# State contributions of the first token half, formed under the second half's convolution units

## The chip, the core and the metric

The kernel runs on one core of one Trainium2 chip. The core has TensorE for matrix products, VectorE, ScalarE and GpSimd for work on tiles, SyncE for issuing transfers, and sixteen DMA engines. Each engine takes the instructions of its own queue in order; semaphores tie the queues together. The metric is the device time of one execution in microseconds (us).

## The reference

One transformer block: a projection of the normalised tokens, then a pooling mixer beside a bidirectional mLSTM with a short convolution on its queries and keys, then an output projection and a gated feed-forward part. The part that matters here is the recurrent state of the mLSTM and how it is used:

```
px, qx, kx, vx, ox, gx = project(hx, w_in[l], conv_qk[l], gate_bias[l])
pc, qc, kc, vc, oc, gc = project(hc, w_in[l], conv_qk[l], gate_bias[l])
hc_m, st_f, st_b = mlstm_bidir(qc, kc, vc, gc, zero_state(bsz), zero_state(bsz))
hx_m, _, _ = mlstm_bidir(qx, kx, vx, gx, st_f, st_b)
mix_x = jnp.concatenate([pool_x, mlstm_output(hx_m, ox, head_norm[l])], axis=-1) @ w_out[l]
x = x + g1 * mix_x
...
  # per chunk, in mlstm_chunk_scan
  c_new = decay[..., None, None] * c0 + jnp.einsum('bhs,bhsv,bhsd->bhvd', wk, vc, kc)
  n_new = decay[..., None] * n0 + jnp.einsum('bhs,bhsd->bhd', wk, kc)
```

There are 2048 tokens, 256 context tokens, width 1024, 4 heads with keys of 64 and values of 128. All is float32.

## The kernel before, in words

The tokens are worked in chunks of 128: 16 token chunks (0 to 15) and 2 context chunks. What a chunk adds to the states, its *contribution*, does not depend on the states themselves: the values times the weighted keys, one product per head for both directions at once. The states are then linked by a scan over the chunks, once forward and once backward.

The input projection runs in two token halves of 1024 tokens. A *unit* is one 256-column block of the projection for one half, computed by the seven products of a Strassen scheme instead of eight (`unit`, line 648; `product`, line 637: 12 matmuls each, as every operand is split in a high and a low part; the loop order of the products is 0, 1, 4, 3, 5, 2, 6, called A0, A1, A4 and so on below). In the second half four of the seven weight operands are not formed anew: they were kept in DRAM in the first half (`s_w`) and are loaded (line 597). These loads are issued only after the last load of raw weights (`issue_after(raw_last)`, line 596).

The second half runs in this order: pool units; two conv units (keys, then queries; their outputs go to DRAM as `s_k`, `s_q`, line 754); then two *o-units* (output gates), interleaved product by product. For the second o-unit the raw weights go into a tile `rawx` of its own (line 691, 1024 columns).

During the o-units a hook after every product (`chunk_step`) works the state contributions of all 18 chunks, two context chunks first, then token chunks in the order 0, 15, 1, 14, ... For each: a load of keys and values one step ahead (lines 897 and 899), two transposes of the keys on TensorE (line 945), a weighting on VectorE (line 948), four matmuls into PSUM (line 958), four copies of [64, 258] on ScalarE into the state tiles (line 963), and, once a chunk of the upper half is reached, a step of the scan on VectorE (line 968). There are 14 hooks; what is left of the 18 chunks follows behind the units. Then the output weights w_out are loaded, scaled and split for the later projection (lines 978 to 994), partly while the mLSTM loop begins.

The mLSTM loop goes chunk by chunk: keys times queries (line 1090), exponentials of the decay matrix (1097), product with them (1099), outputs `po` from values (1114) and from states (1120), normalisation (1132), loads of pool outputs `pmx` (1146) and output gates `so` (1143), and the projection (1171 to 1173).

The program lines give the logical order; a scheduler then lays each engine's queue out in a fixed order, so that work of several stages is mixed in a queue. A wait at the head of a queue holds up all that stands behind it.

Of the kernel before, what the change touches and what calls it, by code (L numbers as in the profile page):

```python
# [8 lines left out]
F32 = mybir.dt.float32  # L9
# [3 lines left out]
ALU = mybir.AluOpType  # L13
# [8 lines left out]
def tile_hybrid_block(ctx: ExitStack, tc: tile.TileContext, x, c, cx, c_ctx, w_ada, b_ada, norm1, w_in, conv_qk,  # L22
                      gate_bias, pool_w, pool_scale, head_norm, w_out, norm2, w_up, w_down, norm_f, out):
    nc = tc.nc
    P = 128
# [100 lines left out]
    s_g = dram.tile([4, D], F32, name="s_g")  # L126
    s_w = dram.tile([6, 4, 2, P, 512], F32, name="s_w")
    s_e = dram.tile([NCH // 2, P, 512], F32, name="s_e")

# [563 lines left out]
    def run_units(units, psp, wp, tmp, fetch, bg=None):  # L695


        for n, (srcs, sink, after, w, half) in enumerate(units):
            if half:
                make = operands(load_raws(srcs, kept=True), [wp], kept=s_w[w])  # L700
            else:
                make = operands(load_raws(srcs), [wp], keep_=s_w[w])
            A = {}
            for j, i in enumerate(ORDER):
                A[i] = make(i)
                if n == 0 and Btile[j] is None:
                    fetch(j)
            for j, _ in enumerate(unit(A, psp, tmp, sink)):
                if bg and (n, j) in bg:
                    bg.pop((n, j))()  # L710
            after()
# [15 lines left out]
    def conv_unit(bp, half, i0):  # L727
        pre = [bp.tile([P, TH + 3], F32, name=f"pre{r}") for r in range(2)]
        for r in range(2):
            if half == 0:  # L730
                nc.gpsimd.memset(pre[r][:, 1:2], 0.0)
            else:
                nc.gpsimd.tensor_copy(pre[r][:, 0:2], edge[:, i0 + r])
                nc.gpsimd.memset(pre[r][:, TH + 2:TH + 3], 0.0)

        def sink(r, n, ps, sb):
            o = pre[r][:, 2 + n * 512:2 + (n + 1) * 512]
            if sb is None:
                nc.scalar.copy(o, ps)
            else:  # L740
                nc.vector.tensor_tensor(o, ps, sb, op=ALU.add)

        def after():
            for r in (0, 1):
                i = i0 + r
                rows = (s_q, s_k)[i // 2][i % 2 * P:(i % 2 + 1) * P]
                y = bp.tile([P, TH + 1], F32, name="y", bufs=2)
                if half == 0:
                    nc.gpsimd.tensor_copy(edge[:, i], pre[r][:, TH:TH + 2])
                    n, o, t0 = TH - 1, 1, 0  # L750
                else:
                    n, o, t0 = TH + 1, 0, TH - 1
                conv_silu(y[:, :n], pre[r][:, o:], n, conv_w(i), y[:, :n])
                nc.sync.dma_start(rows[:, t0:t0 + n], y[:, :n])
        return in_cols(O_Q + i0 * P), sink, after, i0 // 2, half
# [70 lines left out]
    def o_unit(tmp, half, i0):  # L826
# [8 lines left out]
            nc.scalar.dma_start(s_so[i * P:(i + 1) * P, b * 512:(b + 1) * 512], so)  # L835
        return in_cols(O_O + i0 * P), sink, lambda: None, 4 + i0 // 2, half

    for half in range(2):
        if half:
            Btile = [None] * 7  # L840

        def fetch(j):
            if ORDER[j] < 3:
                load_B(s_hc, j, None, None)
            else:
                load_B(s_ha[half], j, wp, "hst")
        if half == 0:
            padr = ExitStack()
            adr = padr.enter_context(pool("adr2", 1))
            fins = []  # L850

            def acc(seg, n):
                return lambda: fins.append(ada_acc(seg, n, adr, 5))

            def fin():
                fins.pop()(tp, "tp")
            with pool("cvp", 1) as bp:
                run_units([conv_unit(bp, half, i0) for i0 in (2, 0)], pu_, wp, tmp, fetch, {(1, 0): acc(3, 0)})
            with pool("gp", 1) as gp:
                GI = gp.tile([P, P], F32, name="GI")  # L860
                GF = gp.tile([P, P], F32, name="GF")
                gates_to(gat, GI, GF, NCH, 64)


                mask = gat.rearrange("p c g -> p (c g)").rearrange("p (d j) -> p d j", d=2)
                nc.gpsimd.memset(mask, 0.0)
                nc.gpsimd.affine_select(out=mask[:, 0], in_=mask[:, 0], pattern=[[1, P]], compare_op=ALU.is_ge, fill=-BIG, base=0,
                                        channel_multiplier=-1)
                nc.gpsimd.affine_select(out=mask[:, 1], in_=mask[:, 1], pattern=[[-1, P]], compare_op=ALU.is_ge, fill=-BIG, base=0,
                                        channel_multiplier=1)  # L870

                gates = gate_chain(gp, gps, GI, GF, P, NCH, False)
                step = lambda: next(gates, None)
                run_units([o_unit(tmp, half, i0) for i0 in (0, 2)], pu_, wp, tmp, fetch,
                          {(0, 0): step, (0, 2): fin, (0, 3): acc(3, 1), (0, 4): step, (1, 0): step, (1, 2): fin,
                           (1, 3): acc(4, 0), (1, 4): step})
            plp = ExitStack()
            plu = pool_units(plp.enter_context(pool("plp", 1)))
            run_units(plu(0), pu_, wp, tmp, fetch, {(0, 3): fin, (0, 4): acc(4, 1), (1, 5): fin})
        else:  # L880
            run_units(plu(1), pu_, wp, tmp, fetch, {(0, 3): acc(2, 0), (1, 3): fin, (1, 4): acc(2, 1)})
            plp.close()
            rxp = pf.enter_context(pool("rx", 1, "right"))
            with pool("cvp", 1) as bp:
                run_units([conv_unit(bp, half, i0) for i0 in (2, 0)], pu_, wp, tmp, fetch, {(0, 3): fin})
            padr.close()
    tpp.close()

# [6 lines left out]
    def dma_kv(kp, sk, sv, cc, bufs, vp=None):  # L895
        kT = kp.tile([P, 2, P], F32, name="kT", bufs=bufs)
        nc.sync.dma_start(kT, sk[:, cc * P:(cc + 1) * P].rearrange("(t p) c -> p t c", p=P))
        vt = vp.tile([P, 4, 129], F32, name="vta", bufs=2) if vp else vtp.tile([P, 4, 129], F32, name="vt")
        nc.sync.dma_start(vt.rearrange("p h v -> p (h v)"), sv[cc * P:(cc + 1) * P, :])
        return kT, vt  # L900
# [5 lines left out]
    bp = pj.enter_context(pool("pja", 1))  # L906
    tmps = (tmp, bp)

    seq = [(True, cc) for cc in range(NCC)] + [(False, cc) for i in range(NCH // 2) for cc in (i, NCH - 1 - i)]
    todo_kv, loaded = list(seq), []  # L910

    def load_ahead():
        if todo_kv:
            is_ctx, cc = todo_kv.pop(0)
            src = (s_kc, s_vc) if is_ctx else (s_k, s_v)
            kp = bp if not is_ctx and len(todo_kv) < 12 and len(todo_kv) % 4 < 2 else kvp
            loaded.append(dma_kv(kp, *src, cc, 2, kvp if is_ctx or cc in (0, NCH - 1) else None))

    for _ in range(2):
        load_ahead()  # L920
# [15 lines left out]
    def ST(k):  # L936
        return sta[:, TA.index(k)] if k in TA else stb[:, TB.index(k)] if k in TB else stc[:, k - 7]
# [628 lines left out]
```

## Time and profile before

| what | value |
|---|---|
| median of 3 runs | 2119.07 us (2118.11 to 2120.87) |
| profiled execution, its own time | 2117.76 us |
| its span in the profile | 2115.9 us |
| mean granted TensorE clock | 0.982 of full speed |
| busy: TensorE, VectorE, ScalarE, GpSimd | 95%, 65%, 42%, 11% |
| chain that ended last: TensorE, DMA, VectorE, ScalarE | 74%, 11%, 5%, 4% |

The span runs from the first to the last recorded instruction; the execution's own time is 1.9 us more. TensorE is busy for nearly the whole span, so the places where it is not busy are what a change in order can win or lose. The page's slices show the granted clock in tenths; where TensorE is idle for long the clock falls, and it is shown for each stage below.

### The profile page before, as it was taken

How to read it: one execution, taken by the hardware profiler on the slowest of the kernel's cores; microseconds unless marked ns; L12 is line 12 of the kernel's file. 1: busy time of each engine (PE TensorE's matmuls, PEld its weight loads, DVE VectorE, ACT ScalarE, POOL GpSimd, SP SyncE). 2: the span in 40 equal slices, each digit the busy share in tenths (PEclk: the TensorE clock that was granted, in tenths of full speed). 3: DMA queues.
4: the chain of work that ended last, by engine and by line, in shares of the span. 5: the costliest groups of instructions: out<-in, count | busy, mean ns of one | idle time of the engine just before them, and what ended most of it. 6: DMA issues, size and time to landing. Idle time of an engine off the chain costs nothing.

```text
span 2115.9 us, 27589 instructions
## 1 busy us (share of the span) xinstructions
PE 2015.6 (95%) x9482; PEld 1637.0 (77%) x9482; DVE 1365.8 (65%) x2333; ACT 899.1 (42%) x1787; POOL 227.0 (11%) x222
## 2 busy tenths in 40 slices
PE   7999989996999998999999999999999999999998
PEld 3997757775777776788888877888888788888887
DVE  6866868757455566666675588677677554447664
ACT  6643644456444444433333354333333343433442
POOL 1000013211333320000000000000000002004121
PEclk9999999997999999999999999999999999999999
DMA  8598989689586756433342367555565584644642
GB/s 281 169 297 270 301 269 329 219 262 254 138 253 209 241 184 183 140 124 125 100 159 85 100 217 256 189 194 189 174 199 192 190 309 149 226 139 168 226 158 100
DMA packets 365812, 421.42 MB, mean 199 GB/s; under 512 B 23924, under 2 KB 241624, under 8 KB 364904
## 3 DMA queue, kind: packets, MB, share of 16 engines
q1 hardware_dynamic: 319728, 348.22, 50.9%
q10 hardware_dynamic: 45944, 71.43, 10.5%
q8 instruction: 75, 1.23, 0.2%
q14 instruction: 65, 0.53, 0.1%
HBM read 280.45 MB, written 139.12 MB: 198 GB/s over the span
## 4 chain that ended last, share of the span: by engine, by line
PE 74%; DMA 11%; DVE 5%; ACT 4%; issue 3%; SPq 1%; POOL 1%; ACTq 0%; DVEq 0%; POOLq 0%
PE pa L642 8%; PE pa L644 8%; PE pa L643 8%; PE pdn L1392 7%; PE pdn L1393 7%; PE pdn L1394 7%; PE pg L642 4%; PE pg L643 4%; PE pg L644 4%; PE pb L642 2%; PE pb L644 2%; PE pb L643 2%; PE pm L1171 2%; PE pm L1173 2%; PE pm L1172 2%
## 5 line engine op out<-in xcount | busy, mean ns | idle before, releaser
L642 PE MATMUL pa<-h,wh 128*128 128x512 f32 x680 | 271.0, 400 | 7.6 <-ACT p L656 4.7
L644 PE MATMUL pa<-h,wl 128*128 128x512 f32 x680 | 269.8, 397 | 0.3 <-DMA wl<-s_w 0.3
L643 PE MATMUL pa<-h,wh 128*128 128x512 f32 x680 | 269.5, 397 | 0.0
L148 ACT CAST wh<-ws 128x512 fp32r<-128x512 f32 x200 | 123.5, 619 | 281.3 <-PE pg L643 154.2
L1392 PE MATMUL pdn<-ow,op 128*128 128x512 f32 x616 | 236.8, 389 | 1.0 <-ACT op L148 1.0
L1393 PE MATMUL pdn<-ow,op 128*128 128x512 f32 x616 | 237.5, 389 | 0.0
L1394 PE MATMUL pdn<-ow,op 128*128 128x512 f32 x616 | 237.5, 389 | 0.0
L151 DVE TENSOR_TENSOR op<-ra,op 128x512 fp32r<-128x512 f32 x154 | 121.6, 796 | 159.4 <-ACT op L148 159.3
L148 ACT CAST op<-ra 128x512 fp32r<-128x512 f32 x154 | 95.2, 621 | 225.9 <-PE pdn L1394 223.9
L642 PE MATMUL pg<-h,wh 128*128 128x512 f32 x448 | 177.8, 397 | 2.9 <-ACT h L148 1.7
L643 PE MATMUL pg<-h,wh 128*128 128x512 f32 x448 | 178.6, 399 | 0.9 <-DVE h L151 0.8
L644 PE MATMUL pg<-h,wl 128*128 128x512 f32 x448 | 177.5, 396 | 0.0
L151 DVE TENSOR_TENSOR wl<-ws,wh 128x512 fp32r<-128x512 f32 x200 | 136.4, 685 | 55.4 <-ACT wh L148 55.2
L642 PEld LDWEIGHTS pa<-h,wh 128*128 128x128 f32 x680 | 129.0, 190 | 43.2 <-ACT p L656 6.0
L644 PEld LDWEIGHTS pa<-h,wl 128*128 128x128 f32 x680 | 128.5, 189 | 31.1 <-issue 0.5
L643 PEld LDWEIGHTS pa<-h,wh 128*128 128x128 f32 x680 | 128.8, 189 | 30.2 <-issue 1.0
L1424 POOL TENSOR_TENSOR hr<-hr,o 128x1024 f32<-128x1024 f32 x8 | 21.7, 2734 | 1096.7 <-ACT o L1437 927.0
L1392 PEld LDWEIGHTS pdn<-ow,op 128*128 128x128 f32 x616 | 115.6, 188 | 25.5 <-ACT op L148 1.4
L1393 PEld LDWEIGHTS pdn<-ow,op 128*128 128x128 f32 x616 | 115.7, 188 | 23.9
L1394 PEld LDWEIGHTS pdn<-ow,op 128*128 128x128 f32 x616 | 115.7, 188 | 23.9
L613 DVE TENSOR_TENSOR ws<-raw 128x512 f32<-128x512 f32 x100 | 69.0, 690 | 96.3 <-DMA raw<-in_w_up_dram 92.0
L148 ACT CAST vt<-raw 128x512 fp32r<-128x512 f32 x112 | 69.2, 619 | 96.0 <-PE pb L643 41.2
(357 smaller groups left out, 4330.5 us busy)
## 6 DMA issues: line engine op xcount, KB each, us to landing
raw<-in_w_up_dram SPq DMA_DIRECT2D x88, 512.0 KB
ra<-s_act SPq DMA_DIRECT2D x66, 512.0 KB
s_act<-adaw SPq DMA_DIRECT2D x84, 256.0 KB
rwt<-s_t SPq DMA_DIRECT2D x77, 256.0 KB
adaw<-in_w_ada_dram SPq DMA_DIRECT2D x64, 256.0 KB
s_act<-g SPq DMA_DIRECT2D x63, 256.0 KB
s_hb<-hb SPq DMA_DIRECT2D x7, 1792.0 KB
hst<-s_hb ACTq DMA_DIRECT2D x48, 256.0 KB
```

The lines of the kernel that those rows point to most:

```text
L148: nc.scalar.copy(hi, src)
L151: eng_lo.tensor_tensor(lo, src, r32(hi), op=ALU.subtract)
L613: nc.vector.tensor_tensor(t, a, b, op=op)
L642: nc.tensor.matmul(ps, lhsT=ah[:, k], rhs=B[:, 0, k], start=st, stop=False, **kw)
L643: nc.tensor.matmul(ps, lhsT=ah[:, k], rhs=B[:, 1, k], start=False, stop=False, **kw)
L644: mm_last[0] = nc.tensor.matmul(ps, lhsT=al[:, k], rhs=B[:, 0, k], start=False, stop=(k == 3), **kw)
L1171: nc.tensor.matmul(pt, lhsT=mh[:, k], rhs=w[:, 0, k % 4], start=(k == 0), stop=False)
L1172: nc.tensor.matmul(pt, lhsT=mh[:, k], rhs=w[:, 1, k % 4], start=False, stop=False)
L1173: nc.tensor.matmul(pt, lhsT=mlo[:, k], rhs=w[:, 0, k % 4], start=False, stop=(k == 7))
L1392: nc.tensor.matmul(ps, lhsT=A[:, 0, ts_], rhs=W[:, 0], start=start, stop=False)
L1393: nc.tensor.matmul(ps, lhsT=A[:, 0, ts_], rhs=W[:, 1], start=False, stop=False)
L1394: nc.tensor.matmul(ps, lhsT=A[:, 1, ts_], rhs=W[:, 0], start=False, stop=stop)
```

## The change

For the chunks 0 to 6 the contribution is formed earlier, by hooks in the two conv units of the second half, and stored in a DRAM tensor `s_d`. When the later chunk step reaches the mirrored upper chunk, the two halves of the stored contribution are loaded straight into the state tiles. The step list shrinks from 18 to 11: two context chunks, 15 to 9, 7 and 8.

```
+    NE = NCH // 2 - 1
+    s_d = dram.tile([NE, P, 516], F32, name="s_d")
...
+    def early_states(room):
...
+        def load():
+            if todo_e:
+                cc = todo_e.pop(0)
+                kT = room[:, cc % 2 * 256:cc % 2 * 256 + 256].rearrange("p (t c) -> p t c", t=2)
+                nc.sync.dma_start(kT, s_k[:, cc * P:(cc + 1) * P].rearrange("(t p) c -> p t c", p=P))
+                vt = wp.tile([P, 4, 129], F32, name="hst", bufs=3)
+                nc.sync.dma_start(vt.rearrange("p h v -> p (h v)"), s_v[cc * P:(cc + 1) * P, :])
...
+                pds = [tp.tile([P, 512], F32, name="tp") for _ in range(2)]
+                for h in range(4):
+                    hh = h % 2 * 129
+                    nc.tensor.matmul(pds[h // 2][:, hh:hh + 129], lhsT=kw[:, h].rearrange("p d c -> p (d c)"),
+                                     rhs=vt[:, h, :], start=True, stop=True)
+                dt = room[:, 512:1028]
+                for p_ in range(2):
+                    nc.scalar.copy(dt[:, 258 * p_:258 * p_ + 258], pds[p_][:, 0:258])
+                nc.sync.dma_start(s_d[cc], dt)
...
-                run_units([conv_unit(bp, half, i0) for i0 in (2, 0)], pu_, wp, tmp, fetch, {(0, 3): fin})
+                estep = early_states(rxp.tile([P, 1028], F32, name="rawx"))
+                bg = {(n, j): estep for n, js in enumerate(((0, 2, 4, 6), (0, 2, 4, 5))) for j in js}
+                bg[0, 3] = fin
+                run_units([conv_unit(bp, half, i0) for i0 in (2, 0)], pu_, wp, tmp, fetch, bg)
...
-    seq = [(True, cc) for cc in range(NCC)] + [(False, cc) for i in range(NCH // 2) for cc in (i, NCH - 1 - i)]
+    seq = [(True, cc) for cc in range(NCC)] + [(False, cc) for cc in range(NCH - 1, NCH // 2, -1)]
+    seq += [(False, NE), (False, NCH // 2)]
...
+            e = NCH - 1 - cc
+            if not is_ctx and e < NE:
+                nc.sync.dma_start(ST(e + 1)[0:64].rearrange("p h v -> p (h v)"), s_d[e, 0:64])
+                if e:
+                    nc.sync.dma_start(ST(NCH - e)[64:128].rearrange("p h v -> p (h v)"), s_d[e, 64:128])
```

The tile handed to `early_states` has the name "rawx" in a pool with one buffer of that name. It is thus the same place in SBUF that the second o-unit's raw weights are loaded into. Its columns 0 to 511 hold two sets of keys, columns 512 to 1027 the one staging area `dt` from which each store to `s_d` is made.

Line numbers move: 597, 691, 754 and 897 of before are 600, 694, 757 and 948 of after; 945, 958, 963, 984, 988 and 1146 are 1003, 1016, 1021, 1042, 1046 and 1204. New lines are 850 and 852 (early loads), 861 (transposes), 863 (weighting), 873 (matmuls), 877 (copies), 878 (stores), 973 and 975 (loads from `s_d`).

Three places of the queues follow, each in the kernel before and in the changed one.

SyncE's queue of before around the load of the second o-unit's raw weights (`rawx<-in_w_in_dram`); `wh<-s_w` and `wl<-s_w` are the kept operands, `kT` and `vta` keys and values of the chunk steps:

```order
L597 DMA wh<-s_w 128x512
L597 DMA wl<-s_w 128x512
L547 DMA s_g<-adacc 1x512
L691 DMA rawx<-in_w_in_dram 128x4x128
L897 DMA kT<-s_kc 128x2x128
L899 DMA vta<-s_vc 128x516
L897 DMA kT<-s_kc 128x2x128
L899 DMA vta<-s_vc 128x516
L691 DMA raw<-in_w_in_dram 128x8x128
```

The load stands early, ahead of the conv outputs' stores, and kept operands follow at once behind the conv unit's.

SyncE's queue of the changed kernel around the same load; `s_d<-rawx` are the stores of contributions, `h` from `s_d` are loads into state tiles:

```order
L948 DMA kT<-s_k 128x2x128 x2
L975 DMA h_4578<-s_d 64x516
L1046 DMA wos<-in_w_out_dram 128x512
L878 DMA s_d<-rawx 128x516
L1046 DMA wos<-in_w_out_dram 128x512
L878 DMA s_d<-rawx 128x516 x2
L694 DMA rawx<-in_w_in_dram 128x4x128
L950 DMA vta<-s_v 128x516
L600 DMA wh<-s_w 128x512
L600 DMA wl<-s_w 128x512
L600 DMA wh<-s_w 128x512
```

The load of the raw weights, and every kept operand of the o-units behind it, now stands behind the last store of a contribution.

TensorE's queue of before between the end of the last conv unit (the third row ends the product A6 on B operand `h_3699`) and the o-units' first kept-weight product A4 (`h_3629`):

```order
L642 MATMUL pa<-h_3699,wh 128x512
L643 MATMUL pa<-h_3699,wh 128x512
L644 MATMUL pa<-h_3699,wl 128x512
L642 MATMUL pa<-h_3629,wh 128x512
L643 MATMUL pa<-h_3629,wh 128x512
L945 MATMUL pb<-ident,kT 128x128 x2
L958 MATMUL pd<-vta,kw 128x129 x4
L644 MATMUL pa<-h_3629,wl 128x512
L642 MATMUL pa<-h_3629,wh 128x512
L643 MATMUL pa<-h_3629,wh 128x512
L644 MATMUL pa<-h_3629,wl 128x512
```

Between the two there is nothing; one transpose pair and four matmuls stand inside A4.

TensorE's queue of the changed kernel between the end of the product A0 of the second o-unit, which is the row ahead of these, and the same product A4 (`h_3630`); `tp<-hst,ws` are the early matmuls, `pd<-vta,kw` those of the context chunks:

```order
L861 MATMUL gps<-ident,rawx 128x128 x2
L873 MATMUL tp<-hst,ws 128x129 x2
L1003 MATMUL pb<-ident,kT 128x128 x2
L873 MATMUL tp<-hst,ws 128x129 x2
L861 MATMUL gps<-ident,rawx 128x128 x2
L1003 MATMUL gps<-ident,kT 128x128 x2
L873 MATMUL tp<-hst,ws 128x129 x4
L1003 MATMUL gps<-ident,kT 128x128 x2
L873 MATMUL tp<-hst,ws 128x129 x8
L1016 MATMUL pd<-vta,kw 128x129 x8
L1003 MATMUL pb<-ident,kT 128x128 x2
L645 MATMUL pa<-h_3630,wh 128x512
```

The matmuls of the early chunks 3 to 6 and those of both context chunks now stand ahead of A4. Behind A4 there are 144 matmuls of the o-units.

ScalarE's queue of before at the last state copies and the loop's first loads: `pmx` is a load of pool outputs, `mh<-pmx` its cast, `h<-big` the cast of a scaled piece of w_out:

```order
L963 COPY h_4459<-pd 64x258
L1143 DMA so<-s_so 128x4x128
L963 COPY h_4458<-pd 64x258
L963 COPY h_4459<-pd 64x258
L1097 ACTIVATE raw<-raw,tokq 128x128 x8
L148 CAST h_5291<-big 128x512 x2
L1097 ACTIVATE raw<-raw,tokq 128x128 x8
L1146 DMA pmx<-s_pm 128x4x128
L1149 DMA big<-in_x_dram 128x1024
L1143 DMA so<-s_so 128x4x128
L1146 DMA pmx<-s_pm 128x4x128
L148 CAST mh<-pmx 128x512
```

The loads of w_out all stand further ahead, among the state copies; the first `pmx` load stands behind the last two of their casts.

ScalarE's queue of the changed kernel from the first exponentials of the loop (line 1155) on:

```order
L1155 ACTIVATE raw<-raw,tokq 128x128 x15
L151 CAST h_5231<-big 128x512
L1155 ACTIVATE raw<-raw,tokq 128x128
L151 CAST h_5231<-big 128x512
L1204 DMA pmx<-s_pm 128x4x128
L1201 DMA so<-s_so 128x4x128
L151 CAST h_5231<-big 128x512
L1204 DMA pmx<-s_pm 128x4x128
L151 CAST h_5231<-big 128x512
L1036 DMA big<-s_g 128x512
L151 CAST mh<-pmx 128x512 x2
L1042 DMA big<-in_w_out_dram 128x2x512
```

The first `pmx` load now stands behind two casts of w_out, and the second pair of w_out pieces is issued behind the casts of the first pair and of `pmx`.

## Rows read from the trace of the kernel before

**Rows 1.** Windows by stage: busy us of each engine, TensorE clock, DMA share, GB/s.

```profile
407.30:427.60 20.30, 20.05 (x99) 16.41 (x97) 13.38 (x16) 13.16 (x20) 3.09 (x5) 1.00 0.65 197
427.60:469.90 42.30, 42.10 (x206) 34.31 (x206) 22.69 (x41) 20.58 (x42) 5.78 (x4) 1.00 0.90 280
469.90:507.80 37.90, 22.26 (x109) 19.16 (x108) 25.77 (x50) 25.73 (x63) 2.79 (x2) 0.73 0.90 231
507.80:529.90 22.10, 12.94 (x61) 9.50 (x61) 18.38 (x45) 12.13 (x40) 5.10 (x3) 0.84 0.88 257
```

**Rows 2.** TensorE's timeline: start, us, engine, line, op, tiles, shape, count [idle before].

```profile
407.29 0.40 PE L642 MATMUL pa<-h,wh 128*128 128x512 f32 x1
...
415.42 0.40 PE L644 MATMUL pg<-h,wl 128*128 128x512 f32 x1
...
427.63 0.50 PE L644 MATMUL pa<-h,wl 128*128 128x512 f32 x1 [0.28 <-DMA wl<-s_w]
...
469.52 0.40 PE L644 MATMUL pa<-h,wl 128*128 128x512 f32 x1
...
478.37 4.04 PE L958 MATMUL pd<-vt,kw 128*128 128x129 f32 x16 [4.02 <-ACT h L963]
...
529.88 3.53 PE L1114 MATMUL po<-vt,raw 128*128 128x129 f32 x16 [0.34 <-DVE h L1132]
...
562.04 2.02 PE L1114 MATMUL po<-vt,raw 128*128 128x129 f32 x16 [0.28 <-DVE h L1132]
```

**Rows 3.** The chain of waits that ended last: start, us, what.

```profile
260.89 2.39 DMA s_w<-wh
...
399.27 4.30 DMA s_pm<-pd
...
420.34 0.23 PE pa L644
...
422.45 5.13 DMA wl<-s_w
...
433.11 0.89 PE pd L958 x8
...
448.24 0.23 PE pb L945 x2
...
492.22 7.14 DMA big<-in_w_out_dram
```

**Rows 4.** SyncE's queue, timeline: the loads that an o-unit waits for.

```profile
400.98 0.38 SPq L691 DMA_DIRECT2D rawx<-in_w_in_dram  x1
...
421.54 0.32 SPq L597 DMA_DIRECT2D wh<-s_w  x1
...
422.45 0.46 SPq L597 DMA_DIRECT2D wl<-s_w  x1
```

**Rows 5.** ScalarE's timeline, conv end, first o-halves, start-up.

```profile
425.85 0.59 ACT L739 COPY pre<-pa 128x512 f32<-128x512 f32 x1 [1.12 <-PE pa L644]
...
426.52 1.15 ACT L471 ACTIVATE y<-pre,vecs 128x1025 f32<-128x1025 f32 x1
...
476.98 0.68 ACTq L984 DMA_DIRECT2D big<-in_w_out_dram  x1
...
487.00 0.62 ACT L148 CAST h<-big 128x512 fp32r<-128x512 f32 x1
...
510.07 0.37 ACTq L1146 DMA_DIRECT2D pmx<-s_pm  x1
...
514.15 0.62 ACT L148 CAST mh<-pmx 128x512 fp32r<-128x512 f32 x1
```

**Rows 6.** The state copies, all of line 963: min/median/max ns, first and last start.

```profile
L963 ACT COPY h<-pd x60: 351/369/372, 433.6 to 507.8; 64x258 f32<-64x258 f32 x60
```

**Rows 7.** VectorE's timeline: w_out scaling, and before the second po group.

```profile
484.85 1.30 DVE L993 TENSOR_TENSOR big<-big 128x512 f32<-128x512 f32 x2 [3.33 <-DMA big<-in_w_out_dram]
...
524.49 0.34 DVE L1132 SCALAR_TENSOR_TENSOR h<-po,rr,hf 128x128 f32<-128x128 f32 x1
```

More of the change, by code (lines that the diff above doesn't have):

```diff
@@ L836, in o_unit, with estep @@
         return in_cols(O_O + i0 * P), sink, lambda: None, 4 + i0 // 2, half
+    def early_states(room):
+        todo_e, got, begun = list(range(NE)), [], []
+        def load():
[5 more added lines that the diff above has]
+                nc.sync.dma_start(vt.rearrange("p h v -> p (h v)"), s_v[cc * P:(cc + 1) * P, :])
+                got.append((cc, kT, vt))
+        def estep():
+            new = None
+            if got:
+                cc, kT, vt = got.pop(0)
+                pk = gps.tile([P, 512], F32, name="gps")
+                for p_ in range(2):
+                    nc.tensor.transpose(out=pk[:, p_ * P:(p_ + 1) * P], in_=kT[:, p_, :], identity=ident)
+                kw = wp.tile([P, 4, 2, 64], F32, name="ws", bufs=3)
+                nc.vector.tensor_tensor(
+                    kw, pk[:, 0:256].rearrange("p (h d) -> p h d", h=4)[:, :, None, :].to_broadcast([P, 4, 2, 64]),
+                    tokq[:, 1, :, :, cc].rearrange("p d h -> p h d")[:, :, :, None].to_broadcast([P, 4, 2, 64]),
+                    op=ALU.mult)
+                new = (cc, kw, vt)
+            if begun:
+                cc, kw, vt = begun.pop(0)
+                pds = [tp.tile([P, 512], F32, name="tp") for _ in range(2)]
[4 more added lines that the diff above has]
+                dt = room[:, 512:1028]
+                for p_ in range(2):
+                    nc.scalar.copy(dt[:, 258 * p_:258 * p_ + 258], pds[p_][:, 0:258])
+                nc.sync.dma_start(s_d[cc], dt)
+            if new:
+                begun.append(new)
+            load()
+        for _ in range(2):
+            load()
+        return estep
     for half in range(2):
@@ L915, in load_ahead @@
             src = (s_kc, s_vc) if is_ctx else (s_k, s_v)
-            kp = bp if not is_ctx and len(todo_kv) < 12 and len(todo_kv) % 4 < 2 else kvp
-            loaded.append(dma_kv(kp, *src, cc, 2, kvp if is_ctx or cc in (0, NCH - 1) else None))
+            kp = bp if not is_ctx and len(todo_kv) < 5 and len(todo_kv) % 4 < 2 else kvp
+            loaded.append(dma_kv(kp, *src, cc, 2, kvp if is_ctx or cc >= NCH - 2 else None))
+            e = NCH - 1 - cc
[3 more added lines that the diff above has]
+                    nc.sync.dma_start(ST(NCH - e)[64:128].rearrange("p h v -> p (h v)"), s_d[e, 64:128])
     for _ in range(2):
```

## The prediction

> **What bounds the kernel now.** I read the windows by stage first [rows 1]. In the conv stage (to 427.6) TensorE is busy 20.05 of 20.30 us, in the o-units' stage (to 469.9) 42.10 of 42.30, both at clock 1.00: nothing but TensorE bounds them, and the DMA engines are 65% and 90% busy beside it. In the third window, the state steps that are left over behind the o-units, it is busy 22.26 of 37.90 us at clock 0.73, and in the start-up of the mLSTM loop 12.94 of 22.10 at 0.84. Only these two stretches, 60.0 us together from the last o-product (469.52 plus its 0.40) to the second po group at 529.88 [rows 2], can be shortened. Then come the holes in them: TensorE's timeline shows a 4.02 us wait for state copies [rows 2], VectorE's a 3.33 us wait for w_out [rows 7], and the chain of waits a 7.14 us load of w_out [rows 3]. So the leftover steps are bound by ScalarE's copies (60 of 0.37 us from 433.6 on [rows 6]) and w_out, not by TensorE. The last views are the queues just ahead: the raw weights of the second o-unit are issued at 400.98, 27 us before the first kept operand is needed; that operand, issued at 422.45, lands 5.13 us later and costs a hole of 0.28 us [rows 2 to 4].
>
> **The change, part by part.** I follow it to one comparable point, the second po group; from there on both programs do the same work and TensorE bounds them, with 16 matmuls of po at 2.02 us in the steady loop and 3.53 us at that point [rows 2], so a shift there is the shift of the end.
>
> Step 1, work moved. Seven chunks leave the steps behind conv: each 4 float32 matmuls (recorded as 8, 0.89 us), one transpose pair (0.23 us) [rows 3] and 4 copies of 0.37 us [rows 6]. Moved under a stage in which TensorE has 0.25 us to spare [rows 1], the 1.12 us of a chunk on TensorE are not hidden but paid there instead. The copies become 14 of [128, 258] instead of 28 of [64, 258]. I take 0.4 us for one: between the 0.37 of a state copy and the 0.59 of a 512-column copy [rows 5, 6], near the first since the columns are equal. ScalarE is busy 13.16 of 20.30 in conv [rows 1], which hides them. The stores (7 of 258 KB) and the loads back (13 of 129 KB) are 1.8 and 1.7 MB more traffic; at 197 to 280 GB/s [rows 1] that is 9 and 6 us of the DMA's time, hidden unless somebody waits.
>
> Step 2, a wait added. Somebody does. The staging area is single, so a chunk's copies wait until the store of the chunk before has landed; and it shares its place with the second o-unit's raw weights, whose load therefore waits for the last store. In SyncE's order that load and every kept operand of both o-units stand behind it. On TensorE the first product that needs one, A4, stands behind the A0 products; nothing else of the o-units can run ahead of it. So a hole opens between them, which before was 0.28 us.
>
> When does A4 start? From 407.29 there are 72 matmuls to the end of conv's last product, at 0.2323 us (35 steps from 407.29 to 415.42 [rows 2]): 16.7; early work among them, four transpose pairs and 2.5 chunks of matmuls and two short ones, 0.9 + 2.2 + 0.5 = 3.6. That gives 427.7. ScalarE then copies the product (0.6) and makes the last conv output (1.15) [rows 5]: 429.5; behind these stand the two copies of chunk 2 (0.8): 430.4. Four rounds follow for chunks 3 to 6, each a store's issue (0.3), its landing L, and two copies (0.8). Then the last store (0.3 + L), four issues on SyncE of 0.32 to 0.46, taken as 0.42 (raw weights, values, the two operands [rows 4]), 1.7, and the operand's own landing.
>
> L is not in the trace before. Near 256 KB between SBUF and DRAM I find 2.39 us for a store in the quiet, 4.30 for one at the end of the pool units, and 5.13 for a load in the o-stage [rows 3]. In the hole itself TensorE asks for little, but the three loads of the o-units, w_out pieces and the states run there. I take 3.4, midway of the two stores, and keep 2.39 and 5.13 as ends. The rounds are 4 × 4.5 = 18.0: 448.4; last store 452.1; issues 453.8; landing **457.2**. With 2.39 it is 451.1, with 5.13 467.6.
>
> The Trainium skill, in "DMA: Bandwidth & Descriptors", section "Anatomy of one DMA — SWDGE (gpsimd) path", gives a fixed cost of about 2.0 us and 436 GB/s beside it; for 258 KB I work out 2.6 us, an estimate from that page. It lies near the quiet row of 2.39 and far below 4.30 and 5.13 [rows 3], where the trace differs; by the page A4 would start at 452.4 and the sum below would come to +0.3 us.
>
> Step 3, the o-stage behind the hole. 144 matmuls × 0.2323 = 33.5, and the contributions still left that stand among them, seven chunks of 1.12 = 7.8: 41.3. (The same count for before, 154 matmuls with five chunks' matmuls and six transpose pairs, gives 41.6 against 42.3 measured.) After a hole of some 25 us TensorE starts at a lower clock: the same 16 po matmuls took 3.53 us after the start-up window (clock 0.84) and 2.02 in the loop [rows 1, 2], 1.5 us more, which I add once: 42.8. The o-stage ends at 500.0, against 469.9.
>
> Step 4, what goes. The leftover state steps behind the o-units vanish nearly whole: of 37.9 us there remain four matmuls or so. But w_out was loaded under them. Its four double pieces were issued from 476.5 on and arrived within the tail; now the load, the scaling and the casts stand in the start-up. In ScalarE's order the first pmx load waits behind two casts of w_out, and the second pair of w_out behind the cast of that pmx. Counted along it from the last o-product to the second po group: 7.1 to the issue of the second double piece (469.9 to 476.98), 7.9 until VectorE takes it up (484.85), 2.8 to the end of its casts (487.62), 4.1 from the pmx load to its cast (510.07 to 514.15), 1.6 for two casts and an issue, 7.1 for the next w_out load, 1.4 for its scaling, 5.4 from the first chunk's normalisation to the second po (524.49 to 529.88) [rows 3, 5, 7]: 37.4. If nothing waits for w_out it is 7.1 plus the 22.1 of the start-up window [rows 1], 29. I take 35, near the counted path, less a little since fewer loads compete.
>
> Sum: 457.2 + 42.8 + 35 = 535.0, against 529.88 before: **+5.1 us**. The profiled execution, 2117.76, becomes 2122.9; the median of the runs is 1.3 higher, so that the forecast is 2124.2. Low end: 451.1 + 41.3 + 29 = 521.4, that is -8.5, 2110.6. High end: 467.6 + 42.8 + 35 = 545.4, +15.5, 2134.6.
>
> **Rivals.**
> 1. *Faster: the short tail wins.* 25 us (60 less 35) go out of tail and start-up, against a hole that the quiet store's 2.39 us makes only 23 us long (427.7 to 451.1). For it: the DMA has no kept operands to load while the hole lasts, and the tail is the only stretch at clock 0.73 [rows 1]. Against it: w_out's 7 to 8 us loads remain [rows 3, 7]. It decides where A4's start plus the rest falls below 529.88: with 42.8 and 29 below 458.1, with 42.8 and 35 below 452.1. Its time is the low end, 2110.6.
> 2. *No change.* Stores land in about 2.6 us, the start-up stays bound by w_out: +0.3, 2119.4. For it: TensorE's whole work is the same, moved and not removed. Against it: the two busier rows of [rows 3].
> 3. *Much slower.* Every store lands like the kept operand, 5.13 us [rows 3], because w_out pieces, state loads and values run in the same window at a DMA share near 0.90 [rows 1]: A4 at 467.6, +15.5, 2134.6. From L above 4.2 the loss passes 10 us (L is in the sum six times, so each 0.1 us of it costs 0.6).
> 4. *The change does not do what it says.* Only chunks 0 to 2 are formed under conv; four of seven fall behind it in TensorE's order. This is no case with a time of its own: it is why the hole has four rounds.
>
> **How the numbers follow.** No change means within 0.2%, 4.2 us, which is about what a measurement of this kernel can tell. The forecast (+5, its own range +1 to +9 from L between 2.9 and 4.1) has 0.45; of it 0.30 lies beyond 4.2 and 0.15 within. Much slower has 0.17, no change 0.18, faster 0.20. So slower is 0.30 + 0.17 = 0.47, same 0.15 + 0.18 = 0.33, faster 0.20. The range 2112 to 2136 leaves out the far part of the faster case and a little above the high end.
>
> **What would show it.** In the profile after: SyncE issues the raw weights of the second o-unit near 452 instead of 401; TensorE has a hole between some 433 and 457 with a granted clock below 1, broken by the early matmuls; the early copies wait each for a store of a contribution, 4 us apart; the o-units end near 500 with no state steps behind them; the second po group starts near 535, and the first pmx and the second pair of w_out are issued after 515. Stores that land in under 2.6 us, or a second po group less than 31 us after the o-units, would make the forecast wrong towards faster; kept operands that take more than 5 us, or an early chunk whose keys come late, towards slower.

## The result, and the profile after

The changed kernel takes 2146.69 us (median of 4 runs, 2142.93 to 2148.66) against 2119.44 for the kernel before beside it (2118.11 to 2120.87): ratio 1.0123, 95% interval 1.0108 to 1.0138. It is slower by 27 us, where 5 were forecast and 2136 was the top of the range.

The windows by stage of the changed kernel are cut where the prediction cuts them: from conv's A1 product to the start of the hole, the hole, the o-units behind it, and from the last o-product to the second po group. The columns are those of [rows 1].

```profile
407.90:436.60 28.70, 28.67 (x134) 23.44 (x135) 18.70 (x23) 16.09 (x24) 2.84 (x5) 0.94 0.63 188
436.60:465.80 29.20, 13.22 (x60) 10.92 (x58) 7.19 (x13) 7.26 (x19) 2.34 (x1) 0.60 0.74 226
465.80:509.20 43.40, 43.36 (x216) 36.34 (x217) 22.55 (x47) 20.42 (x43) 3.40 (x3) 0.95 0.72 229
509.20:557.80 48.60, 20.77 (x81) 15.14 (x80) 35.79 (x72) 25.75 (x70) 9.18 (x6) 0.66 0.89 243
```

The last window is called the start-up from here on. The second row is the new hole: TensorE is busy 13.2 of 29.2 us at clock 0.60. The third is the o-units at full work. The fourth is 11.4 us shorter than the 60.0 of before, but TensorE is idle 27.8 us in it, more than the 24.8 of before. TensorE's timeline of the changed kernel gives the points that answer to [rows 2]:

```profile
407.92 0.50 PE L645 MATMUL pb<-h,vt 128*128 128x512 f32 x1 [3.25 <-DVE pre L744]
...
448.79 2.09 PE L873 MATMUL tp<-hst,ws 128*128 128x129 f32 x8 [4.27 <-ACT rawx L877]
453.82 2.09 PE L873 MATMUL tp<-hst,ws 128*128 128x129 f32 x8 [2.94 <-ACT rawx L877]
...
465.84 0.79 PE L645 MATMUL pa<-h,wh 128*128 128x512 f32 x1 [2.37 <-DMA wh<-s_w]
...
508.78 0.39 PE L647 MATMUL pa<-h,wl 128*128 128x512 f32 x1
...
555.89 2.08 PE L1148 MATMUL pqk<-h,kT 128*128 128x256 f32 x4 [6.77 <-DMA h<-s_q]
557.76 3.65 PE L1172 MATMUL po<-vt,raw 128*128 128x129 f32 x16
```

The second po group stands at 557.76 against 529.88: 27.9 us late, the whole loss. The sum in the prediction had 535.0 there. SyncE's queue of the changed kernel, with the stores and what follows them (it answers to [rows 4]):

```profile
421.62 0.32 SPq L878 DMA_DIRECT2D s_d<-rawx  x1
...
430.63 0.39 SPq L878 DMA_DIRECT2D s_d<-rawx  x1
...
442.47 0.32 SPq L878 DMA_DIRECT2D s_d<-rawx  x1
...
449.50 0.39 SPq L878 DMA_DIRECT2D s_d<-rawx  x1
...
460.45 0.38 SPq L694 DMA_DIRECT2D rawx<-in_w_in_dram  x1
...
461.43 0.42 SPq L600 DMA_DIRECT2D wh<-s_w  x1
```

The raw weights, at 400.98 in [rows 4], are now issued at 460.45. The chain of waits of the changed kernel, from 430 to 466, is the row of stores itself:

```profile
430.63 5.47 DMA s_d<-rawx
436.12 0.66 ACT rawx L877 x2
436.79 4.91 DMA s_d<-rawx
442.47 5.79 DMA s_d<-rawx
...
449.50 3.79 DMA s_d<-rawx
454.07 3.15 DMA s_d<-rawx
458.00 2.31 DMA s_d<-rawx
...
461.43 4.36 DMA wh<-s_w
```

Six stores one behind the other, 4.2 us each on average, 25.4 of the 36 us. The later ones are quicker, and the DMA engines are less busy around them: their share is 0.96 from 430 to 440, 1.00 from 440 to 450 and 0.40 from 450 to 460.

### The profile page after: what moved, and what is told of

Same layout as the page of the kernel before. It is cut to its first block, busy times and chain, and to the rows that moved or that the text cites. A ratio compares the mean times of both kernels' runs of the same rounds, so it can differ in the third digit from the quotient of the medians.

```text
span 2146.5 us, 27592 instructions
## 1 busy us (share of the span) xinstructions
PE 2024.1 (94%) x9482; PEld 1642.4 (77%) x9482; DVE 1366.6 (64%) x2333; ACT 893.3 (42%) x1775; POOL 224.4 (10%) x222
## 4 chain that ended last, share of the span: by engine, by line
PE 72%; DMA 13%; DVE 5%; ACT 4%; issue 3%; SPq 1%; POOL 1%; ACTq 0%; DVEq 0%; POOLq 0%
PE pa L645 8%; PE pa L646 8%; PE pa L647 8%; PE pdn L1450 7%; PE pdn L1452 7%; PE pdn L1451 6%; PE pg L646 4%; PE pg L647 4%; PE pg L645 4%; PE pb L645 2%; PE pb L647 2%; PE pb L646 2%; PE pm L1229 2%; PE pm L1231 2%; PE pm L1230 2%
## 5 line engine op out<-in xcount | busy, mean ns | idle before, releaser
L1229 PE MATMUL pm<-h,mh 128*128 128x512 f32 x256 | 107.2, 419 | 5.7 <-ACT mh L151 4.5
```

The lines of the kernel that those rows point to most:

```text
L1229: nc.tensor.matmul(pt, lhsT=mh[:, k], rhs=w[:, 0, k % 4], start=(k == 0), stop=False)
```

## The experiments

Each is an edit of the changed kernel, of e2, or of the kernel before, as said. The code shows the lines that matter; "..." stands for lines left out. A ratio is the time against the kernel before beside it, with its 95% interval.

**e1, keys apart.** The early keys go to the three buffers named "ws", which the early weighted keys use as well.

```
-                kT = room[:, cc % 2 * 256:cc % 2 * 256 + 256].rearrange("p (t c) -> p t c", t=2)
+                kT = wp.tile([P, 4, P], F32, name="ws", bufs=3)[:, 0:2]
```

> Control for the next two: only the early chunks' keys go to other buffers; the one staging area stays, and still in the place of the second o-unit's raw weights. In TensorE's order chunk 0's matmuls stand about three products (8 us) earlier. If the hole ahead of A4 is the row of seven stores, each landing (4.2 us on average) before the next copies, the row starts and ends 8 us earlier: A4 near 458, time near 2139. If the row is paced by the keys' loads in SyncE's queue it gains more, below 2133. If neither, 2147. From the last o-product to the second po group nothing changes: 48.6 us, give or take 3.

2131.84 us, ratio to before 1.0060 (1.0042 to 1.0078). The seven stores start at 406.0 instead of 421.6 and end at 439.4 instead of 458.0; the raw weights are issued at 441.84. The row is hardly shorter (33.4 us against 36.4), it only starts earlier, by 15.6 us. The raw weights come 18.6 us earlier and the time falls by 14.9, so the time follows the end of the row. The start moved by twice the 8 us expected, and the time is below the 2133 that the expectation gave to the keys: their buffers in the shared place had held back the row's start.

**e2, own place.** As e1, and the staging area no longer lies where the raw weights go (they need only half of their tile).

```
-                st = other.tile([P, KD, P], F32, name="rawx")
+                st = other.tile([P, 4, P], F32, name="rawx")
...
-                dt = room[:, 512:1028]
+                dt = room[:, 0:516]
...
-                estep = early_states(rxp.tile([P, 1028], F32, name="rawx"))
+                estep = early_states(rxp.tile([P, 516], F32, name="est"))
```

> As e1, but the second o-unit's raw weights have a place of their own, so these weights and the kept operands are not behind the stores; the staging area is still single. Theory 'place' (the hole is the weights' wait for the last store): A4 starts behind A0 near 432, the o-units end near 478, second po near 525, time near 2114. Rival 'row of stores' (TensorE meets the matmuls of chunks 4 to 6 inside the o-units' products and waits there for the stores all the same): time only as e1, 2135 to 2140. From the last o-product to the second po: 48 us by the theory that DMA bytes bound it (same bytes), under 40 by the theory that w_out's queue order bounds it and the earlier loads help.

2122.68 us, 1.0015 (1.0004 to 1.0026): 24 us less than the changed kernel. A4 starts at 433.43:

```profile
433.43 0.51 PE L645 MATMUL pa<-h,wh 128*128 128x512 f32 x1 [2.47 <-DMA wh<-s_w]
```

That is what 'place' expects. Its 2114 is missed, because the o-units then take until 485.8: the early work and all state steps stand among their products. TensorE's account, from 400 to the last o-product and from there to the second po, first of before and then of e2:

```profile
400.00:469.90 69.90, 67.97 (x329) 55.15 (x327) 39.48 (x61) 36.63 (x64) 9.25 (x13) 1.00 0.83 255
469.90:529.90 60.00, 35.20 (x170) 28.66 (x169) 44.16 (x94) 37.87 (x102) 7.89 (x5) 0.77 0.89 240
```

```profile
400.00:485.80 85.80, 79.42 (x410) 65.05 (x408) 48.08 (x81) 42.90 (x82) 10.33 (x13) 1.00 0.89 275
485.80:531.80 46.00, 21.51 (x88) 17.07 (x89) 34.50 (x73) 26.43 (x74) 8.55 (x6) 0.70 0.98 244
```

The second stretch is 14.0 us shorter and has 13.7 us less TensorE work in it. Its idle time, 24.5 us, is what it was (24.8), and the work comes back in the first stretch, which is longer by 15.9 (11.5 of work, the rest idle).

**e3, two stagings.** As e1, with the staging area doubled, in the shared place.

```
-                dt = room[:, 512:1028]
+                dt = room[:, cc % 2 * 516:cc % 2 * 516 + 516]
...
-                estep = early_states(rxp.tile([P, 1028], F32, name="rawx"))
+                estep = early_states(rxp.tile([P, 1032], F32, name="rawx"))
```

> As e1, but two staging areas in turn, still in the place of the raw weights. 'Row of stores': two stores are under way at a time, last store lands near 442, A4 near 450, time near 2130. 'Place': as e1, 2139, since the weights stand behind the last store in any case. Both effects together would put it between, and e2 lower.

2130.09 us, 1.0052 (1.0034 to 1.0070), the time of the 'row of stores' but not its reason: against e1 the raw weights come only 1.6 us earlier (440.25), the time is the same within the intervals, which is what 'place' says (as e1). With the keys apart, the copies of e3 wait for TensorE's matmuls (4.0 us), not for stores. Here a second staging area was worth little, as the last store still stood ahead of the weights.

**e4, no late scan.** The scan steps of the mLSTM loop's first half are left out of the changed kernel.

```
-        if t < NCH // 2 - 1:
-            scan_step(NCH // 2 + t)
```

> The changed kernel without the seven scan steps (28 VectorE instructions of 0.35 us) of the mLSTM loop's first half; the states of the upper chunks are then not linked. Theory 'VectorE bounds the start-up' (it is busy 10.0 and 9.2 of 10 us in 530 to 550): from the last o-product to the second po 48.6 falls by about 10. Theory 'DMA bytes bound it' (11.8 MB at 243 GB/s, as 14.4 MB at 240 in 60.0 us before): it stays at 48.6, give or take 2.

2136.74 us in one run. From the last o-product to the second po it takes 33.9 us instead of 48.6, at the same 244 GB/s, with 8.3 MB. That is more than the 9.8 us of VectorE's work. But TensorE's order differs here: three *key products* (keys times queries of one chunk, line 1148) stand ahead of the second po instead of five, and fewer loads with them. So e4 alone decides between neither theory.

**e5, x later.** On e2; the load of x moves from the preparation of a chunk to its projection.

```
-        with tc.issue_after(copies[-4].ins):
-            nc.scalar.dma_start(xt, x[csl, :])
...
+        nc.scalar.dma_start(xt, x[csl, :])
```

> As e2, but the token rows x of a chunk (512 KB) are loaded one chunk step later, at the projection instead of its preparation; TensorE's order is the same, instruction for instruction. In e2 the second po group starts 46.0 us behind the last o-product, with 11.2 MB at 244 GB/s in that time. Theory 'bytes' (the DMA rate bounds the start-up): three loads, 1.57 MB, leave it, 6 us less, 40. Theory 'VectorE' (its queue of scan steps and w_out work): 46, give or take 1. Theory 'w_out chain' (two loads of w_out one behind the other): 46, or 1 to 2 less by faster landings.

2123.39 us, 1.0018 (0.9998 to 1.0037); 49.5 us in the start-up, with 11.4 MB. The loads did not leave the stretch, so this tells nothing on the bytes.

**e6, scan on GpSimd.** On e2; the seven late scan steps as multiplications and additions of [128, 258] on GpSimd.

```
+        if k > 7:
+            for i in (0, 2):
+                t_ = m2.tile([P, 2, 129], F32, name="sct", bufs=1)
+                nc.gpsimd.tensor_tensor(t_, a[:, i:i + 2], decx[:, i:i + 2, k:k + 1].to_broadcast([P, 2, 129]), op=ALU.mult)
+                nc.gpsimd.tensor_tensor(b[:, i:i + 2], b[:, i:i + 2], t_, op=ALU.add)
+            return
```

> As e2, but the seven late scan steps go from VectorE to GpSimd (28 VectorE instructions out, 28 GpSimd ones in); TensorE's order is the same. 'VectorE': 28 x 0.35 = 9.8 us leave its queue, start-up 36 to 38, time near 2113. 'Bytes' and 'w_out chain': 46, time near 2122. A GpSimd step that is slower than 2 us per chunk would hold up the po groups instead: above 46.

The start-up falls from 46.0 to 36.3 us, and VectorE's busy time in it from 34.5 to 25.6 us. A scan step takes some 3.3 us on GpSimd, and the po groups were not held up by it as the expectation feared. But TensorE's order is not the same as expected: four key products stand ahead of the second po, five in e2 (the table below comes back to it). And the time is 2124.67, 1.0033 (1.0015 to 1.0051). TensorE's timeline of e6, behind the second po at 526.96:

```profile
526.96 2.05 PE L1178 MATMUL po<-vt,raw 128*128 128x129 f32 x16 [0.87 <-DVE h L1196]
...
554.63 0.50 PE L1235 MATMUL pm<-h,mh 128*128 128x512 f32 x1 [1.81 <-ACT mh L151]
...
573.23 1.97 PE L293 MATMUL pm<-ident,big 128*128 128x128 f32 x8 [4.06 <-DVE big L1248]
```

The lead of 7.3 us over e2 at the third po group is 0.9 at the fourth and gone at the fifth: waits for a cast of pmx and for VectorE take its place, with a lower clock behind them (0.89 from 550 to 580, in e2 1.00).

**e7, half of w_out.** On e2.

```
-                    nc.scalar.dma_start(st2, w_out[k * P:(k + 2) * P, ns].rearrange("(e p) c -> p e c", e=2))
+                    nc.scalar.dma_start(st2[:, 0], w_out[k * P:(k + 1) * P, ns])
-                st = st2[:, kk % 2]
+                st = st2[:, 0]
```

> As e2, but of each double piece of w_out only the first half is loaded and used twice (half of the projection's lower weights is then the wrong half); TensorE's order is the same. 'Bytes': 1.05 MB less at 244 GB/s, 4.3 us less. 'w_out chain': two loads of 7 to 8 us become some 4.5 each, 5 to 6 us less. 'VectorE': no change. With e5 it tells bytes (both fall) from the chain (only e7 falls).

2121.84 us, 1.0017 (1.0001 to 1.0034); start-up 45.3 us against 46.0. The windows of the start-up in e7, and in e12 (below):

```profile
484.40:529.80 45.40, 21.57 (x90) 16.55 (x90) 34.56 (x72) 26.26 (x73) 9.68 (x6) 0.70 0.81 221
```

```profile
486.20:527.30 41.10, 20.55 (x86) 15.61 (x85) 29.40 (x54) 23.68 (x64) 18.09 (x17) 0.66 0.97 258
```

In e7 the DMA share falls from 0.98 to 0.81 and the rate from 244 to 221 GB/s, and the stretch stays: halving these loads, 1.2 MB less, is worth 0.7 us. So neither these bytes nor the length of the two loads of w_out set it.

**e8, three chunks.** As e2, with the chunks 0 to 2 alone formed early.

```
-    NE = NCH // 2 - 1
+    NE = 3
...
-    seq = [(True, cc) for cc in range(NCC)] + [(False, cc) for cc in range(NCH - 1, NCH // 2, -1)]
+    seq = [(True, cc) for cc in range(NCC)] + [(False, cc) for cc in range(NCH - 1, NCH - 1 - NE, -1)]
-    seq += [(False, NE), (False, NCH // 2)]
+    seq += [(False, cc) for i in range(NE, NCH // 2) for cc in (i, NCH - 1 - i)]
```

> As e2, but only the chunks 0 to 2 are formed early, the others in pairs as before. Theory 'TensorE's work is only moved' (what the tail loses, conv and o-units gain, and the idle 25 us belong to the start-up): time as before, 2118 to 2121, whatever the number of chunks. Rival 'each early chunk saves its idle share of the tail': half way between before and e2 without e2's stalls, below 2116.

2123.11 us, 1.0018 (1.0000 to 1.0035): 2 us above what 'only moved' expects, and far from the rival's 2116. Start-up 50.7 us with 29.7 of TensorE work.

**e9, no stores.** The changed kernel with the line of the store (878) left out.

```
-                nc.sync.dma_start(s_d[cc], dt)
...
-                nc.sync.dma_start(ST(e + 1)[0:64].rearrange("p h v -> p (h v)"), s_d[e, 0:64])
+                nc.sync.dma_start(ST(e + 1)[0:64].rearrange("p h v -> p (h v)"), s_v[e * P:e * P + 64, :])
...
```

> The changed kernel without the seven stores; the state tiles are loaded from the values instead of the stored contributions (as many bytes, wrong numbers). The place is still shared with the second o-unit's raw weights. 'Row of stores': copies no longer wait, chunk 6's are done near 441, the raw weights are issued there instead of at 460, the o-units end near 492 as in e1, time 2128 to 2134. If it is the keys' loads or the DMA load that pace the row, the raw weights stay behind 452 and the time above 2140. The start-up is 46 to 49 us in either case.

2129.02 us, 1.0065 (1.0049 to 1.0082), as 'row of stores' expected; the start-up, 42.3 us, is shorter than the 46 to 49 expected. The copies of e9, and its load of the raw weights:

```profile
L877 ACT COPY rawx<-tp x14: 353/374/387, 420.3 to 442.4; 128x258 f32<-128x258 f32 x14
```

```profile
443.26 0.41 SPq L694 DMA_DIRECT2D rawx<-in_w_in_dram  x1
```

The first copy is where it was (420.3 against 420.9), the last comes at 442.4 instead of 457.6, and the raw weights are issued at once. The time is 17.7 us less than the changed kernel's. With the waits, e9 also leaves out the traffic of the stores, 1.8 MB, which it cannot tell apart from them.

**e10 and e11, the kernel before with late scan steps on GpSimd**, all seven and the first three (the edit of e6; in e11 with `if 7 < k < 11:`).

> The kernel before with its seven late scan steps on GpSimd (as e6). If VectorE's queue bounds the 60.0 us from the last o-product to the second po group, the idle 24.8 us of TensorE in it fall by up to 9.8, the second po stands near 521. Whether the time follows: 2110 if the next groups of the loop keep the lead, 2118 to 2122 if they give it back to waits for pmx and the lower clock, as in e6 (po groups 2 to 5 against e2: -4.9, -7.3, -0.9, +2.0).

> The kernel before with only the first three late scan steps on GpSimd. VectorE theory: 12 x 0.35 = 4.2 us out of its queue, second po near 526; with less for GpSimd to do beside its mask additions the lead should last longer: 2114 to 2117. Rival (no lead lasts): 2118 to 2120.

2127.28 us, 1.0042 (1.0017 to 1.0067), and 2120.91, 1.0016 (1.0000 to 1.0033). From the last o-product to the second po both take 57.5 us instead of 60.0, e10 with 10.5 us less VectorE work in it and 25.8 us idle on TensorE. Seven steps give no more than three, so the scan steps are worth 2.5 us there at most; and as four key products stand ahead of the second po in both and five in the kernel before, even that can be the order. The trace of e10 shows what takes their place (ScalarE, VectorE, TensorE):

```profile
526.62 0.31 ACT L1140 ACTIVATE hf<-h 128x128 f32<-128x128 f32 x1 [5.10 <-DMA big<-in_x_dram]
...
527.31 0.35 DVE L1138 SCALAR_TENSOR_TENSOR h<-po,rr,hf 128x128 f32<-128x128 f32 x1 [5.40 <-ACT hf L1137]
...
528.79 3.81 PE L1120 MATMUL po<-vt,raw 128*128 128x129 f32 x16 [5.92 <-DVE h L1138]
```

The second po waits for VectorE's normalisation of the first, VectorE for ScalarE, and ScalarE's queue, by the profile, for a load of x.

**e12, e2 with three scan steps on GpSimd.**

> e2 with the first three late scan steps on GpSimd: second po about 4 us earlier than in e2 (531.8), time near 2118 to 2120 if the lead lasts, 2122 as e2 if not. It would have to come out below 2116 to beat both kernels.

2121.12 us, 1.0004 (0.9986 to 1.0023): the best version with early states, and no different from the kernel before. The start-up is 41.1 us, 4.9 less than e2, with four key products ahead of the second po as in e6. No version beat the kernel before.

**The start-ups side by side.** These are the profiled executions, one of each kernel, all but the first with seven early chunks. The last two columns are against the kernel before:

| kernel | key products ahead of the second po | scan steps on GpSimd | start-up, us | second po, us | end of the span, us |
|---|---|---|---|---|---|
| before | 5 | 0 | 60.0 | | |
| changed | 5 | 0 | 48.6 | +27.9 | +30.6 |
| e1 | 5 | 0 | 47.7 | +10.0 | +10.4 |
| e2 | 5 | 0 | 46.0 | +1.9 | +3.0 |
| e3 | 4 | 0 | 42.5 | +2.1 | +12.9 |
| e9 | 4 | 0 | 42.3 | +6.8 | +14.4 |
| e12 | 4 | 3 | 41.1 | -2.6 | -1.2 |
| e6 | 4 | 7 | 36.3 | -2.9 | +3.9 |

e5 and e7, with five key products, took 49.5 and 45.3. So of the 9.7 us between e2 and e6 some 6 belong to the scan steps (42.4 in e3 and e9 to 36.3 in e6, with four key products in each, though e3 and e9 keep the shared place), and the rest goes with the order. The last columns say what a start-up that is shorter by the order alone is worth: e3 and e9 lose 8 to 11 us again behind the second po. It is one point for two kernels only where the same work stands ahead of it.

## Why the prediction was wrong

The direction, the mechanism of the hole and its place were right: A4 behind the last store, the raw weights late, a hole with a lowered clock. The size was not: +5.1 against +27.9 at the second po. Three terms make up the 535.0, and their errors make up the 22.8 us. The step that failed is step 4, "I take 35, near the counted path", by 13.6 us; step 2 was off by 8.6.

*A4's start, 457.2 forecast, 465.84 measured: 8.6 us.* The first error is in "behind these stand the two copies of chunk 2 (0.8): 430.4". These copies ended at 436.8, 6.4 us later. Some 5 of the 6.4 are the conv stage, whose last product ended at 432.8 instead of 427.7. Its first product, A1, began at 407.92; this is its row in the kernel before:

```profile
404.41 0.50 PE L642 MATMUL pb<-h,vt 128*128 128x512 f32 x1 [1.48 <-DVE pre L741]
```

Of the 3.5 us between them, 1.8 were there already at 376, ahead of the first early load (402.33), where nothing of the change has begun: the spread of single executions. The other 1.7 are a longer hole ahead of A1 (3.25 us against 1.48), and A1 itself then took 1.7 us more, at 0.43 us a matmul for its first nine against 0.23. This goes with the changed kernel: in e4 and e9 the hole was 4.03 and 3.52 us, in e10 and e11 0.53 and 0.43. The sum had no term for it.

The rest of the 6.4 is that the step took the store of chunk 1 for landed. ScalarE's queue of the changed kernel shows that it was not even issued:

```profile
425.29 0.38 ACT L877 COPY rawx<-tp 128x258 f32<-128x258 f32 x1
427.80 0.62 ACT L151 CAST wh<-raw 128x512 fp32r<-128x512 f32 x1 [2.13 <-PE pa L646]
428.32 1.06 ACT L477 ACTIVATE y<-y 128x1025 f32<-128x1025 f32 x1
429.28 0.57 ACT L659 COPY p<-pa 128x512 f32<-128x512 f32 x1
429.75 0.38 ACT L877 COPY rawx<-tp 128x258 f32<-128x258 f32 x1
...
436.12 0.65 ACT L877 COPY rawx<-tp 128x258 f32<-128x258 f32 x2 [1.44 <-DMA s_d<-rawx]
```

Chunk 1's two copies lie 4.5 us apart, with a cast, an activation and a product's copy between them. Its store goes out at 430.63 and lands at 436.1, so the row has five rounds, not four. Most of that landing lay under the late conv stage; chunk 2's copies waited for it 1.44 us.

The next four rounds take 21.2 instead of 18.0 us: a landing was 4.4 on average in them, taken as 3.4, within the bounds 2.39 to 5.13. Last store, issues and the operand's landing took 7.9 instead of 8.8. Together 6.4 + 3.2 - 0.9 = 8.7. The lower bound was misread: the 2.39 us are called a store in the quiet, but the DMA engines were busy for 0.88 of that time:

```profile
260.90:263.30 2.40, 2.40 (x13) 1.91 (x13) 2.37 (x5) 1.07 (x2) 0.00 (x0) 1.00 0.88 315
```

So the middle between it and 4.30 (share 0.90) was no price for a busier time; that the mean came out within the bounds was in part luck. e9 and e1 show that the time follows this row, e2 that it does so through the shared place.

*The o-units behind it, 42.8 forecast, 43.3 measured.* Right, the lower clock included (0.95 in that window).

*From the last o-product to the second po, 35 forecast, 48.6 measured: 13.6 us.* This is the larger error. I counted along the w_out loads and took off a little "since fewer loads compete". e7 shows that halving these loads changes 46.0 to 45.3, so their length was not what bounds. VectorE's work in the stretch, by line, in the changed kernel (columns: busy us, mean ns, idle before and its releasers):

```profile
L1026 DVE SCALAR_TENSOR_TENSOR h<-h,decx 128x129 f32<-128x129 f32 x24 | 12.5, 553 | 0.0
L154 DVE TENSOR_TENSOR h<-big,h 128x512 fp32r<-128x512 f32 x8 | 5.3, 679 | 0.0
L1157 DVE TENSOR_TENSOR raw<-raw,pqk 128x1024 f32<-128x1024 f32 x4 | 4.9, 1215 | 2.0 <-DMA kT<-s_k 2.0
L1026 DVE SCALAR_TENSOR_TENSOR h<-h,decx,h 128x129 f32<-128x129 f32 x12 | 3.7, 346 | 0.0
```

16.2 us of scan steps stand in it ahead of, and among, the products (line 1157) that the loop's first groups need. [rows 1] had the warning: VectorE was busy 25.77 of 37.90 and 18.38 of 22.10 us, 44.2 in the 60.0, and in the changed stretch it is busy 35.8, only 8.4 less. Even without a gap these do not fit into 35 us. And they have gaps: VectorE waits 3.7 us for a cast and 3.2 for a load of w_out, and from 524.8, when that load is there, to 552.6 it is busy 26.9 of 27.8 us. How much of the 13.6 us is VectorE's is shown in part: with four key products ahead of the second po, taking all seven scan steps off it shortens the start-up by some 6 us. With five, as in the changed kernel, it is longer by 3 to 7 us, and the last of them waits there 6.77 us for a load of queries (`h<-s_q`). No run takes this fifth product away alone, so its share is argued. I named no rival in which VectorE becomes the bound.

Of the rivals, "much slower" had the right cause for part of it, the stores' landings, but with four rounds and the same 35 us at its end. (Two slips in the working: 429.5 and 0.8 make 430.3, and L between 2.9 and 4.1 gives +2 to +9, not +1.) The estimate of 2.6 us from the Trainium skill ("DMA: Bandwidth & Descriptors", section "Anatomy of one DMA — SWDGE (gpsimd) path") comes from a formula for transfers that GpSimd issues. These stores were issued by SyncE; only the last, 2.31, came in under it, and the others in the row took 3.15 to 5.79.

The idea behind step 4, that the leftover state steps take idle time of TensorE with them, fell with e2: 14.0 us and 13.7 us of work left the stretch, its idle time stayed, and the work was paid for in the stage before. In the changed kernel the idle time even rose, from 24.8 to 27.8. e8, with fewer chunks moved, came out at the same time as e2.

What stays open: which chain sets the 60.0 us of before, as e10 leaves VectorE's scan steps 2.5 us at most and shows a wait of ScalarE close behind; what the order of the key products is worth by itself; and whether fewer bytes would shorten the start-up further, as e5 did not take them out and e7 took 1.2 MB only.

## What to carry to other kernels

Moving work of the busiest engine into a stretch where that engine is full costs its whole length there. It pays only by the idle time that goes from the stretch that it leaves, and in e2 none went. Before a stretch is shortened in a sum, add up every engine's busy time in what will be left in it: the new length can't go below the largest. A point that is compared between two kernels must have the same work ahead of it in both. And a staging area lent from a tile that is needed next puts the last store ahead of that tile's load, and with it of everything in order behind the load; lend from a tile whose next use is far off.

## What the runs showed of the hardware

Stores of 258 KB to DRAM took 2.31 to 5.79 us in one row, longest where the DMA engines were busiest (0.96 to 1.00 of the time from 430 to 450) and shortest where they were less busy (0.40 from 450 to 460). The share alone does not set it: in the kernel before, a store of 256 KB took 2.39 us at a share of 0.88.

GpSimd took 0.62 to 1.17 us for a multiplication or an addition of [128, 258] in e6, so that a scan step of four such took some 3.3 us there against 1.4 on VectorE. VectorE's scan instructions of 0.35 us got longer beside an operation of GpSimd. The longest in the changed kernel's start-up, with what GpSimd did at the time:

```profile
549.61 2.43 DVE L1026 SCALAR_TENSOR_TENSOR h<-h,decx 128x129 f32<-128x129 f32 x1
```

```profile
549.23 2.65 POOL L1150 TENSOR_TENSOR raw<-raw,gat 128x1024 f32<-128x1024 f32 x1 [9.44 <-DMA raw<-s_R]
```

The other long ones there lie beside GpSimd operations at 530.84, 534.98 and 538.40 in the same way, which is why 24 of the scan instructions have a mean of 553 ns and 12 one of 346.

TensorE's granted clock was 0.60 of full speed over the hole, mostly the lower of its two levels (1.2 and 2.4 GHz), with work for 13.2 of 29.2 us; the early matmuls took 2.09 us there against 1.06 for the same eight records at 428.99.
